# Queries, keys and gates of eight retention heads computed as Strassen pairs in a stage of their own and kept in DRAM, in a one-core decoder layer

## The chip, the cores and the metric

The kernel runs on one core of one Trainium2 chip. The metric is the device time of one execution in microseconds (us); lower is better. Times before: 1721.08, 1719.35 and 1719.22 us, median 1719.35.

## What is computed

One layer over 512 prompt tokens and 8 sequences of 8 sample tokens, T = 576 columns in all, with D = 1024 channels. Between two SwiGLU FFNs stands the token mix, which is what the change touches:

```python
z = h @ w_in                       # 1024 x 10240
u, v, q, k, rv, rg, ga, gb = jnp.split(z, SPLIT_POINTS, axis=-1)
u = gelu(u); v = layer_norm(gelu(v))
o_a = u * chunk_spatial_mix(v, gm_ws, gm_bs)
qh, kh = rotary(q), rotary(k) * DK ** -0.5          # 8 heads of 128
o_r, S_new = retention(qh, kh, rv, S0)              # values: 8 heads of 256
o_b = head_rms(o_r) * silu(rg)
merged = sigmoid(ga) * (o_a @ w_a) + sigmoid(gb) * (o_b @ w_b)
x = x + g2 * (merged @ w_o)
```

So q, k, ga and gb are 8 column blocks of 128 each and rg is 16: 48 blocks of `w_in` that all multiply the same normalised, modulated input.

## The kernel before, in words

Channels lie on the 128 partitions and tokens along the free dimension; T is worked in two halves of H = 288 columns. All data is fp32. A product is made of three matmuls, high times high, high times low and low times high, from operands that ACT (high part, a cast) and DVE (low part, a subtraction) split; `proj` (L516 to L526, matmul at L522) makes a 128 x 288 result out of 8 chunks of 128 channels that way, 24 matmuls. A weight block of 128 columns, `load_w`, is one 512 KB load on SP's queue, an ACT cast (L141) and a DVE subtraction (L142).

The program runs in this order:

- **The first FFN.** Its gate and up products go through `Weights`, `Plain` and `Pair`: a pair of weight blocks (gate and up) with both token halves is a 2 x 2 block product, and Strassen's scheme makes it with 7 products of 12 matmuls (L679) in place of 8. The operands (`Operands`) hold the needed sums of the input's blocks. `Plain` uses 8 products and serves the first two strips, while those sums are still being made; `Pair` serves the others. `ada_rest` (matmuls L265) makes the conditioning vectors a strip at a time in the background.
- **The entry to the token mix** (`last_down1`). Its steps stand in a written order, the string `INTO_MIX`. The last down products of the FFN interleave with the RMS norm of the new input, and `Modulate` (L448 to L493) turns it into the operands X, high and low, of all products in the token mix. Head 0's first blocks start here.
- **The heads**, the loop of 8 over `project` (L1196), `core` and `out_b`. `project` makes q, k and two rg blocks of a head with `proj` (8 calls, 192 matmuls), then the values (L1236: 96 matmuls of 128 x 256, L1244 for the sample tokens). `rotary` (L1186 to L1189) takes q and k out of PSUM on DVE and adds on POOL. `core` (L1278 to L1408) is the retention: it is a generator that is started, ticked by other code's products and finished, so that its small matmuls fall between the large ones of the next head's `project` and of `out_b`. It ends with the head's norm: L1377 and L1378 copy and square, L1380 adds, `split` (L149, L150) makes high and low, L1402 sums over partitions with a matrix of ones, L1406 and L1407 multiply by the gate and the norm. `out_b(h-1)` makes the 8 blocks of `w_b` (96 matmuls) and DVE adds each into `acc` in SBUF (L1421).
- **The gated branch.** `values(0)`, `values(1)` (L1452), a layer norm, then `mix(g)` (L1560, L1564) between the `gate_u` products, with the eight `gate_b` blocks filling in; a mix ends in L1566 and L1570 on DVE, L1574 on POOL, and `split`.
- **The merge.** x1 comes back from DRAM (L1604), the eight ga blocks are made, then `w_a`, then `w_o` in the written order `INTO_FFN2`, which also starts the second FFN with the same `Plain` and `Pair`.

All DMAs are issued on SP's queue; POOL and ACT issue none. The scheduler of the tile framework keeps each engine's program in the order of the code, apart from where generators are ticked.

Of the kernel before, what the change touches and what calls it, by code (L numbers as in the profile page):

```python
# [15 lines left out]
P = 128  # L16
# [15 lines left out]
NSLOT = 28  # L32
# [5 lines left out]
xt0 xt1 xc0 xt2 xc1 xt3 xc2 xt4 xc3 s5 xt5 xc4 r5 r50 r51 r52 xt6 dg xc5 xt7 xc6 rw xS  # L38
xc7 rr xr0 xr1 mm0 xr2 M0 tr0 xr3 mm1 m0 nh0 s0 M1 nl0 b00 tr1 b01 m1 wh0 tx0 b10 s1 b11
wl0 N11h0 N11h1 N11l0 N1h0 N11l1 mm2 tx1 N1l0 N1h1 h0a0 T2a1 M2 N1l1 nh1 T2a0 wh1 nl1  # L40
tr2 sn0 h1a0 m2 wl1 b20 b21 s2 B21h2 T2b0 B22h2 h0a1 B21l2 T2h0 N3c0 N4c0 N3h0 T2l0 N4h0
N3l0 mm3 N4l0 sn1 B22l2 M3 tr3 h1a1 m3 b30 s3 b31 B21h3 T2b1 p2ah B21l3 p2S h0b1 B22h3
p2bh N4c1 T2h1 p2bl N4h1 T2l1 p2al h0b0 N3c1 B22l3 N3h1 N4l1 N3l1 h1b0 e0s0 e0s1 e0m0
e0m1 h1b1 e1a0 p2Sh e1t0 e1s0 p2Sl e1m0 p2U Gh0 P1 e1t1 p2V e1a1 p2Uh P2 Gl0 e1s1 p2Ul
P1s P5 e1m1 Gh1 P6 Gl1 P5s P6s
"""
INTO_MIX = """
D00 D01 rs00 Wh2 sq00 ad00 Wl2 D10 rs01 px0 Wh3 sq01 ad01 Wl3 D11 rs10 sq10 ad10 Wh6 D20
rs11 Wl6 px1 sq11 ad11 D21 Wh7 rs20 sq20 Wl7 ad20 D30 rs21 Wh4 px2 sq21 Wl4 ad21 D31
rs30 sq30 ad30 Wh5 Wl5 D40 rs31 px3 sq31 wh0 D50 ad31 rs40 sq40 wl0 ad40 D60 rs50 sq50  # L50
wh1 ad50 wl1 D70 rs60 sq60 wh2 ad60 D41 rs70 xa60 wl2 sq70 xa70 ad70 rd0 rs41 D51 wh3
px4 rq0 wl3 sq41 ad41 q00 D61 rs51 q10 px5 sq51 q20 t00 t60 t10 hi00 D71 t70 t20 hi10
lo00 hi20 ad51 lo10 hi60 t30 hi70 lo20 hi30 B00 t40 rs61 hi40 rs71 px6 B10 sq61 lo40 px7
lo30 sq71 ad61 lo70 B20 xa61 t50 xa71 ad71 hi50 B30 lo60 lo50 rd1 B40 rq1 q01 B50 q11
q21 t11 up0 B60 t01 hi11 t21 hi01 lo11 t71 B70 hi21 um0 t61 hi71 lo01 R0 uh00 t41 uh01
ul00 ud0 lo21 hi41 ul01 t31 uc00 up1 uc01 t51 hi31 lo41 hi51 lo31 hi61 um1 lo51 uh10
lo61 ud1 ul10 uh11 lo71 uc10 ul11 uc11
"""
INTO_FFN2 = """
W00 W01 Wh2 rs00 sq00 ad00 Wl2 W10 Wh3 rs01 px0 Wl3 sq01 ad01 W11 Wh4 rs10 sq10 Wl4 ad10  # L60
W20 Wh5 rs11 px1 Wl5 sq11 ad11 W21 Wh6 rs20 sq20 Wl6 ad20 W30 Wh7 rs21 px2 sq21 Wl7 ad21
# [14 lines left out]
def layer_kernel(ctx: ExitStack, tc: tile.TileContext, a):  # L76
# [17 lines left out]
    now = {"xa": xa, "wraw": None, "whl": None}  # L94
    turn = {"wraw": 0, "whl": 0}
# [18 lines left out]

    def weight(tag, shape, dt, bufs):
        turn[tag] += 1
        own = now[tag] is not None and turn[tag] % (bufs + 1) == 0
        return (now[tag] if own else wp).tile(
            [P] + shape, dt, tag=tag, name=nm(tag), bufs=1 if own else bufs
        )  # L120

    def raw4(shape):
        return weight("wraw", shape, F32, 3)

    def whl(shape):
        return weight("whl", shape, F32R, 4)
# [668 lines left out]
    class Pair(Weights):  # L795
# [29 lines left out]
        def Sl(self):  # L825
            self.put_lo(("s3", "s1"))
# [1010 lines left out]
```

## Time and profile before

| | |
|---|---|
| median of three runs | 1719.35 us |
| the profiled execution, its own time | 1718.67 us |
| its span in the trace | 1716.6 us |
| granted TensorE clock, mean | 0.996 |
| busy: PE, DVE, ACT, POOL | 1683.7, 1049.4, 686.6, 209.0 us |
| data moved by DMA | 199.52 MB, mean 116 GB/s |

The profiled execution took 1718.67 us by the same clock as the other runs; its span, from the first to the last instruction in the trace, is 1716.6 us, so 2.07 us lie around it. A row of the groups by line names line, engine, operation, the tiles out<-in, the shape and the count, then busy time in us and the mean ns of one, then the idle time of the engine ahead of them and what ended it. A row of the windows is start:end and length in us, then busy us with the number of instructions of PE, of its weight loads (PEld), DVE, ACT and POOL, the granted clock, the share of the 16 DMA engines, and GB/s. A matmul's mean in a group is longer than the time that it adds, since matmuls are pipelined: busy time over count is the pace.

### The profile page before, as it was taken

What the parts mean: (1) busy time and instruction counts of PE and PEld (TensorE: products, weight loads), DVE (VectorE), ACT (ScalarE), POOL (GpSimd) and SP (SyncE); (2) the same over time, 40 slices, a digit from 0 to 9 for tenths busy, and PEclk for the clock granted to TensorE, in tenths of its full rate; (3) what the DMA queues carried; (4) which work ended last, traced back from release to release, by engine and by line L of the source; (5) the groups of instructions that cost most, each with busy time, mean ns of one, the idle gap of its engine ahead of it and who ended that gap; (6) DMA issues with size and microseconds to landing.
All of it is one profiled execution on the core that took longest, in us unless ns stands there. A gap on an engine that the chain in (4) does not pass through costs nothing.

```text
span 1716.6 us, 30444 instructions
## 1 busy us (share of the span) xinstructions
PE 1683.7 (98%) x12588; PEld 1610.9 (94%) x12588; DVE 1049.4 (61%) x1758; ACT 686.6 (40%) x1137; POOL 209.0 (12%) x263
## 2 busy tenths in 40 slices
PE   7999999999999999999999999999999999999997
PEld 4879999999999999999999889999999999999997
DVE  6856847676765745745745546422547958666773
ACT  5533524335534333333333333322235525344354
POOL 0000000000421302302202101220021000000002
PEclk9999999999999999999999999999999999999999
DMA  9443444323454433444424335342330323323231
GB/s 301 132 145 98 134 139 129 99 87 95 146 163 140 142 115 125 132 123 125 149 83 143 100 115 161 103 154 75 99 103 21 87 80 92 99 84 89 86 99 56
DMA packets 279773, 199.52 MB, mean 116 GB/s; under 512 B 9801, under 2 KB 253769, under 8 KB 279634
## 3 DMA queue, kind: packets, MB, share of 16 engines
q1 hardware_dynamic: 279634, 197.58, 38.4%
q8 instruction: 98, 1.61, 0.4%
q14 instruction: 41, 0.34, 0.1%
HBM read 183.12 MB, written 14.42 MB: 115 GB/s over the span
## 4 chain that ended last, share of the span: by engine, by line
PE 88%; DVE 4%; DMA 4%; ACT 2%; issue 1%; SPq 0%; POOL 0%; POOLq 0%; DVEq 0%; ACTq 0%
PE ps L522 47%; PE ps L679 24%; PE ps L1236 5%; PE ps L1452 3%; PE ps L265 2%; DMA wraw<-in_w_down_dram 1%; DMA ada<-in_w_ada_dram 1%; DVE whl L707 1%; PE ps L1366 1%; PE ps L1244 1%; PE ps L1328 1%; DMA xa<-in_w_ada_dram 1%; ACT whl L697 1%; PE ps L1372 1%; PE ps L1344 0%
## 5 line engine op out<-in xcount | busy, mean ns | idle before, releaser
L522 PE MATMUL ps<-xa,whl 128*128 128x288 f32 x2784 | 378.4, 295 | 0.5 <-DVE whl L142 0.3
L522 PEld LDWEIGHTS ps<-xa,whl 128*128 128x128 f32 x2784 | 370.9, 188 | 7.6 <-issue 3.4
L679 PE MATMUL ps<-xa,whl 128*128 128x288 f32 x2064 | 292.8, 296 | 1.9 <-ACT whl L697 1.0
L679 PEld LDWEIGHTS ps<-xa,whl 128*128 128x128 f32 x2064 | 279.1, 188 | 10.5 <-issue 2.5
L142 DVE TENSOR_TENSOR whl<-wraw,whl 128x1024 fp32r<-128x1024 f32 x100 | 126.2, 1270 | 212.4 <-ACT whl L141 208.4
L522 PE MATMUL ps<-c,wd 128*128 128x288 f32 x1824 | 246.7, 295 | 0.0
L522 PEld LDWEIGHTS ps<-c,wd 128*128 128x128 f32 x1824 | 243.2, 188 | 2.6 <-issue 1.7
L679 PE MATMUL ps<-xs,whl 128*128 128x288 f32 x1680 | 239.7, 296 | 1.6 <-ACT sn L688 1.4
L679 PEld LDWEIGHTS ps<-xs,whl 128*128 128x128 f32 x1680 | 228.5, 188 | 7.5 <-ACT sn L688 4.9
L522 PE MATMUL ps<-c,whl 128*128 128x288 f32 x1368 | 194.9, 298 | 0.0
L522 PEld LDWEIGHTS ps<-c,whl 128*128 128x128 f32 x1368 | 184.1, 188 | 2.7 <-DVE S L1391 0.8
L141 ACT CAST whl<-wraw 128x1024 fp32r<-128x1024 f32 x100 | 104.0, 1046 | 107.3 <-PE ps L522 47.6
L509 POOL TENSOR_TENSOR x<-x,s 128x64 f32<-128x64 f32 x72 | 34.4, 478 | 909.4 <-DVE s L508 909.2
L503 DVE SCALAR_TENSOR_TENSOR x<-ps,gate,x 128x288 f32<-128x288 f32 (+1 forms) x128 | 61.5, 483 | 135.3 <-PE ps L522 134.9
L697 ACT CAST whl<-sum 128x1024 fp32r<-128x1024 f32 x80 | 84.0, 1050 | 86.3 <-DVE sum L832 58.2
L707 DVE TENSOR_TENSOR whl<-sum,whl 128x1024 fp32r<-128x1024 f32 x80 | 98.0, 1225 | 30.2 <-ACT whl L697 28.2
L697 ACT CAST whl<-wraw 128x1024 fp32r<-128x1024 f32 (+1 forms) x84 | 70.6, 841 | 98.5 <-PE ps L679 84.8
L1236 PEld LDWEIGHTS ps<-whl,xa 128*128 128x128 f32 x768 | 94.1, 194 | 5.1 <-DVE whl L142 3.4
L1236 PE MATMUL ps<-whl,xa 128*128 128x256 f32 x768 | 95.6, 286 | 3.2 <-DVE whl L142 3.2
L909 ACT CAST wd<-wraw 128x640 fp32r<-128x640 f32 (+2 forms) x58 | 45.3, 782 | 123.6 <-PE ps L522 116.7
L707 DVE TENSOR_TENSOR whl<-wraw,whl 128x1024 fp32r<-128x1024 f32 (+1 forms) x84 | 81.2, 967 | 9.5 <-ACT whl L697 9.1
L688 ACT COPY sn<-ps 128x288 f32<-128x288 f32 x126 | 50.1, 398 | 59.2 <-PE ps L679 57.7
(264 smaller groups left out, 1835.2 us busy)
## 6 DMA issues: line engine op xcount, KB each, us to landing
wraw<-in_w_in_dram SPq DMA_DIRECT2D x80, 512.0 KB
ada<-in_w_ada_dram SPq DMA_DIRECT2D x56, 512.0 KB
wraw<-in_w_gate_dram SPq DMA_DIRECT2D x88, 256.0 KB
wraw<-in_w_up_dram SPq DMA_DIRECT2D x88, 256.0 KB
wraw<-in_w_down_dram SPq DMA_DIRECT2D x32, 384.0 KB
wraw<-in_w_down_dram SPq DMA_DIRECT2D x32, 320.0 KB
S<-in_state_ret_dram SPq DMA_DIRECT2D x32, 256.0 KB
wraw<-in_w_b_dram SPq DMA_DIRECT2D x16, 512.0 KB
```

Of the source, the lines that this page charges most:

```text
L141: ACT.copy(out=hi, in_=raw)
L142: (eng or DVE).tensor_tensor(out=lo, in0=raw, in1=hi.bitcast(F32), op=ALU.subtract)
L503: DVE.scalar_tensor_tensor(out=x[:, o:o + w], in0=ps[:, :w], scalar=g[:, c, 0:1], in1=x[:, o:o + w], op0=ALU.mult, op1=ALU.add)
L509: return lambda: POOL.tensor_tensor(out=x[:, NP:T], in0=x[:, NP:T], in1=u, op=ALU.add)
L522: PE.matmul(ps[:, :H], lhsT=s[:, k, c0:c0 + P], rhs=m[:, HALF[h]], start=k == 0 and z == 0, stop=k == kc - 1 and z == 2,)
L679: PE.matmul(ps[:, :H], lhsT=s[:, j * P:(j + 1) * P], rhs=m[:, j, :], start=fresh and j == 0 and z == 0, stop=j == 3 and z == 2, skip_group ...
L688: ACT.copy(out=t, in_=ps[:, :H])
L697: ACT.copy(out=hl[:, 0], in_=src)
L707: DVE.tensor_tensor(out=hl[:, 1], in0=src, in1=hl[:, 0].bitcast(F32), op=ALU.subtract)
L909: ACT.copy(out=hl[:, 0], in_=self.raw[c])
L1236: PE.matmul(ps[:, :DV], lhsT=s, rhs=m, start=i == 0, stop=i == 23)
L1452: PE.matmul(ps, lhsT=s, rhs=m[:, kx % 2, :], start=kx == 0 and z == 0, stop=kx == KC - 1 and z == len(terms) - 1,)
```

## The change

The 48 blocks q, k, rg, ga and gb are made as 24 pairs in a stage between the first FFN and the heads. The first two pairs (rg of heads 0 and 1) are `Plain2`, 96 matmuls each; the other 22 are `Pair2`, 84 each. `INTO_MIX` starts the first three of them the way `INTO_FFN2` starts an FFN. A finished block is a tile of 128 x 576 that POOL stores to DRAM (`qkd`, `rgd`, `gad`, `gbd`). The operands of the values are remade in the stage from x1 and the norm's row, both stored to DRAM in the entry (16 DMAs on ACT's queue for x1) and fetched again by POOL; `ada_rest(10..17)` moves into the stage. A head fetches q and k (each also with its partition halves swapped) and rg by SP; DVE and POOL make the rotary on 576 columns in SBUF. `out_b(h)` runs two heads later, ACT copies its sums out of PSUM, and for heads 1 to 7 POOL adds them to `accd` in DRAM with an accumulating DMA; `out_b(7)` is in the loop of mixes. `gates_of` fetches ga, gb and `accd` for `w_a`. The `gate_b` and ga products of the old merge are gone. A pair's sums are made in place in the raw weight tiles, in both FFNs as well. Counted over the program, matmuls of 128 x 288 go from 10116 to 9852, DVE instructions from 1760 to 1798, ACT from 1129 to 1382, and POOL from 268 to 345, 113 of those DMAs of 128 x 576.

The diff, cut to its core:

```diff
-NSLOT = 28
+NSLOT = 33
+NSLOT2 = 7
+SSLOT = 11
...
     class Pair(Weights):
         def S(self):
-            self.sum = now["raw"].tile([P, 2, 512], F32, tag="sum", name=nm("sum"), bufs=1)
-            DVE.tensor_tensor(
-                out=self.sum, in0=self.q[:, 1:2].broadcast_to([P, 2, 512]), in1=self.p, op=ALU.add
-            )
+            DVE.tensor_tensor(out=self.p[:, 1], in0=self.q[:, 1], in1=self.p[:, 1], op=ALU.add)
+            DVE.tensor_tensor(out=self.q[:, 1], in0=self.q[:, 1], in1=self.p[:, 0], op=ALU.add)
...
+    def stream(p, begun=False):
+        if not begun:
+            p.splits()
+            p.p1()
+            p.p1s()
+            p.p2()
+        behind()
+        p.e2()
+        if not begun:
+            p.p5()
+            p.p5s()
+            p.p6()
+            p.p6s()
+        p.p3()
+        p.p7()
+        held.append(p.p4)
...
+    class Kept:
+        def post(self, i, h, src):
+            if self.func:
+                ACT.activation(out=self.out(i, h), in_=src, func=self.func)
+            elif src.tensor is not self[i].tensor:
+                ACT.copy(out=self.out(i, h), in_=src)
+            self.left[i] -= 1
+            if not self.left[i]:
+                POOL.dma_start(out=self.dst(i), in_=self[i])
...
+            steps[f"sp{c}{h}"] = lambda c=c, h=h: nc.scalar.dma_start(out=x1d[:, c, HALF[h]], in_=xs[c][:, HALF[h]])
...
+    start(operands_of_values(), 4.0)
+    start(ada_rest(range(10, 18), 8.0), 9.0)
+    for w in (
+        [qk(hd) for hd in range(1, HEADS)] + [rg(hd) for hd in range(2, HEADS)]
+        + [gb(c) for c in range(0, KC, 2)] + [ga(c) for c in range(0, KC, 2)]
+    ):
+        stream(pair2(w))
+    finish()
...
+    def fetch(hd):
+        rope, t = tks["rope"], []
+        for i in range(2):
+            src = qkd[:, 2 * hd + i]
+            x, y = slot([P, T]), slot([P, T])
+            nc.sync.dma_start(out=x, in_=src)
+            nc.sync.dma_start(out=y[0:64], in_=src[64:128])
+            nc.sync.dma_start(out=y[64:128], in_=src[0:64])
+            t.append((x, y))
+        rg = [slot([P, T]) for _ in range(2)]
+        for e in range(2):
+            nc.sync.dma_start(out=rg[e], in_=rgd[:, 2 * hd + e])
+        for x, y in t:
+            DVE.tensor_tensor(out=x, in0=x, in1=rope[:, 0], op=ALU.mult)
+            DVE.tensor_tensor(out=y, in0=y, in1=rope[:, 1], op=ALU.mult)
+            POOL.tensor_tensor(out=x, in0=x, in1=y, op=ALU.add)
+        return t[0][0], t[1][0], rg
...
+    def out_b(hd, OB, j):
+        wb = load_w(a["w_b"][0], 2 * hd, 2, j * 512, 512)
+        for c in range(4):
+            t = slot([P, T])
+            for h in range(2):
+                ps = proj(wb, OB, h, kc=2, c0=c * P)
+                ACT.copy(out=t[:, HALF[h]], in_=ps[:, :H])
+                tick(cost(2))
+            dst = accd[:, 4 * j + c, :]
+            if hd == 0:
+                nc.sync.dma_start(out=dst, in_=t)
+            else:
+                POOL.dma_start(out=dst, in_=t, accum_op=ALU.add)
...
     for hd in range(HEADS):
-        mine = project(hd)
-        OB = []
-        gen = core(hd, *mine, OB)
-        if prev is not None:
-            finish(prev[0])
-            start(gen, 1.0)
-            out_b(hd - 1, prev[1])
+        if hd == 0:
+            rv, rvs = values_of(hd)
+            q, k, gates = fetch(hd)
         else:
-            start(gen, 1.0)
-        prev = gen, OB
+            q, k, gates = fetch(hd)
+            rv, rvs = values_of(hd)
+        if hd > 1:
+            for j in range(2):
+                out_b(hd - 2, OBs[hd - 2], j)
+        if prev:
+            finish(prev)
+        OBs.append([])
+        prev = core(hd, q, k, gates, rv, rvs, OBs[hd])
+        start(prev, 0.5)
...
+    def gates_of(c):
+        t = [slot([P, T]) for _ in range(3)]
+        for d, src in zip(t, (gad, gbd, accd)):
+            nc.sync.dma_start(out=d, in_=src[:, c])
+        POOL.tensor_tensor(out=t[2], in0=t[2], in1=t[1], op=ALU.mult)
```

How the change moves instructions, at three places. The first is PE at the end of head 0's core. In the kernel before (L1387 the state's products, L1402 the sums for the norm, L522 the next head's projection):

```order
L1387 MATMUL ps_5718<-c_5537,c_5543 128x256 x2
L1387 MATMUL ps_5723<-c_5537,c_5543 128x256 x2
L1387 MATMUL ps_5728<-c_5537,c_5544 128x256 x2
L1387 MATMUL ps_5733<-c_5537,c_5544 128x256 x2
L522 MATMUL ps_5738<-xa_4536,whl_5455 128x288 x6
L522 MATMUL ps_5738<-xa_4537,whl_5455 128x288 x6
L522 MATMUL ps_5738<-xa_4538,whl_5455 128x288 x6
L522 MATMUL ps_5738<-xa_4539,whl_5455 128x288 x6
L1402 MATMUL ps_5768<-c_5714,onesr 128x288
L1402 MATMUL ps_5768<-c_5715,onesr 128x288
L1402 MATMUL ps_5787<-c_5714,onesr 128x288
L1402 MATMUL ps_5787<-c_5715,onesr 128x288
```

In the changed kernel (L1452 the state's products, L1467 the sums for the norm, L1295 the values of the next head):

```order
L1452 MATMUL ps_8783<-c_8599,c_8605 128x256 x2
L1452 MATMUL ps_8788<-c_8599,c_8605 128x256 x2
L1452 MATMUL ps_8793<-c_8599,c_8606 128x256 x2
L1452 MATMUL ps_8798<-c_8599,c_8606 128x256 x2
L1467 MATMUL ps_8807<-c_8779,onesr 128x288
L1467 MATMUL ps_8808<-c_8779,onesr 128x288
L1295 MATMUL ps_8859<-whl_8851,xx_5394 128x256 x6
L1295 MATMUL ps_8859<-whl_8851,xx_5395 128x256 x3
L1467 MATMUL ps_8807<-c_8780,onesr 128x288
L1467 MATMUL ps_8808<-c_8780,onesr 128x288
```

The two sums of the norm stood behind 24 projection matmuls; of head 0's, the first now directly follow the state's products, and the next fill is nine value matmuls.

The second is PE at the last of the mixes. Before (L1560 and L1564 are a mix, L522 on `xa` the gate products around it):

```order
L522 MATMUL ps_12061<-xa_4539,whl_12025 128x288 x6
L1560 MATMUL ps_12089<-gws,c_10953 128x128
L1560 MATMUL ps_12089<-gws,c_10980 128x128
L1560 MATMUL ps_12089<-gws,c_11013 128x128
L1560 MATMUL ps_12089<-gws,c_11048 128x128
L1564 MATMUL ps_12094<-wd_11271,c_11067 128x64
L522 MATMUL ps_12109<-xa_4536,whl_12106 128x288 x6
L522 MATMUL ps_12109<-xa_4537,whl_12106 128x288 x6
L522 MATMUL ps_12109<-xa_4538,whl_12106 128x288 x6
```

In the changed kernel (L447 on `c_12079` is `out_b(7)`, L1633 and L1637 are the mixes, L447 on `c_12655` is the first product of `w_a`, which reads the first mixes' results):

```order
L447 MATMUL ps_13126<-c_12081,whl_13060 128x288
L1633 MATMUL ps_13135<-gws,c_12225 128x128
L1633 MATMUL ps_13135<-gws,c_12252 128x128
L1633 MATMUL ps_13135<-gws,c_12279 128x128
L1633 MATMUL ps_13135<-gws,c_12306 128x128
L1637 MATMUL ps_13140<-wd_12388,c_12325 128x64
L1633 MATMUL ps_13150<-gws,c_12225 128x128
L1633 MATMUL ps_13150<-gws,c_12252 128x128
L1633 MATMUL ps_13150<-gws,c_12279 128x128
L1633 MATMUL ps_13150<-gws,c_12306 128x128
L1637 MATMUL ps_13155<-wd_12388,c_12325 128x64
L447 MATMUL ps_13189<-c_12655,whl_13186 128x288
```

Mixes stood apart by gate products; now mixes 6 and 7 follow each other and `w_a` follows them at once.

The third is POOL in a head. Before (L1189 ends a rotary, L1406 multiplies by the gate, L1282, L1296 and L1299 prepare the sample tokens):

```order
L1189 TENSOR_TENSOR c_8534<-h_8563,h_8564 128x288
L1406 TENSOR_TENSOR h_8582<-c_8417,c_7802 128x288
L1406 TENSOR_TENSOR h_8587<-c_8418,c_7803 128x288
L1406 TENSOR_TENSOR h_8601<-c_8417,c_7802 128x288
L1406 TENSOR_TENSOR h_8606<-c_8418,c_7803 128x288
L1189 TENSOR_TENSOR c_8534<-h_8636,h_8637 128x288
L1282 TENSOR_TENSOR qdS<-c_8534,hc_8980 128x8x8
L1189 TENSOR_TENSOR c_8535<-h_8667,h_8668 128x288
L1189 TENSOR_TENSOR c_8535<-h_8698,h_8699 128x288
L1296 COPY h_9011<-c_8535 128x2x64
L1299 COPY h_9011<-c_8535 128x2x64
L1278 TENSOR_TENSOR c_9001<-c_8534,hc_8980 128x512
```

In the changed kernel (L1481 multiplies by the gate, L1498 are the accumulating DMAs of one `out_b`, L1282 ends the rotary, L1343 and L1384 are the decay products of the core):

```order
L1481 TENSOR_TENSOR c_10992<-c_10992,c_10279 128x576
L1481 TENSOR_TENSOR c_10993<-c_10993,c_10280 128x576
L1498 DMA accd<-c_11015 128x576
L1498 DMA accd<-c_11047 128x576
L1498 DMA accd<-c_11090 128x576
L1498 DMA accd<-c_11108 128x576
L1498 DMA accd<-c_11131 128x576
L1498 DMA accd<-c_11175 128x576
L1498 DMA accd<-c_11193 128x576
L1498 DMA accd<-c_11211 128x576
L1282 TENSOR_TENSOR c_11229<-c_11229,c_11230 128x576
L1343 TENSOR_TENSOR c_11307<-c_10749,hc_11286 128x512
```

POOL's arithmetic is on 576 columns where it was on 288, and the eight DMA issues of an `out_b` stand in its queue ahead of the rotary of a head.

More of the change, by code (lines that the diff above doesn't have):

```diff
@@ L1065, in layer_kernel @@
     run(BEGIN, steps)
-    x1d = dr.tile([P, KC, T], F32, name="x1d")
     n2 = Norm()
@@ new lines, in core @@
+        r = tp.tile([P, T], F32, tag="all", name=nm("r"), bufs=1)
+        u = slot([P, T])
+        for h in range(2):
+            ACT.activation(
+                out=r[:, HALF[h]], in_=ps[h][:, :H], func=AF.Abs_reciprocal_sqrt, scale=1.0 / DV, bias=epsT
+            )
+        DVE.scalar_tensor_tensor(out=u, in0=r, scalar=-0.5 / DV, in1=r, op0=ALU.mult, op1=ALU.mult)
+        for h in range(2):
+            DVE.scalar_tensor_tensor(
+                out=u[:, HALF[h]], in0=ps[h][:, :H], scalar=DV * EPS, in1=u[:, HALF[h]], op0=ALU.add, op1=ALU.mult
+            )
@@ L1707, in tok_end @@
         dst = a["y_prompt"][0, cl] if n < 4 else a["y_sample"].rearrange("b l d -> (b l) d")
[L1708 to L1711 removed]
+        out = raw4([2, 512])
         for i in range(2):
```

623 lines of the change are left out of this document (296 added, 327 removed).

## The prediction

> **What bounds the kernel now.** First the page's head, its chain of waits by engine and its DMA queues:
>
> ```profile
> span 1716.6 us, 30444 instructions
> PE 1683.7 (98%) x12588; PEld 1610.9 (94%) x12588; DVE 1049.4 (61%) x1758; ACT 686.6 (40%) x1137; POOL 209.0 (12%) x263
> PE 88%; DVE 4%; DMA 4%; ACT 2%; issue 1%; SPq 0%; POOL 0%; POOLq 0%; DVEq 0%; ACTq 0%
> q1 hardware_dynamic: 279634, 197.58, 38.4%
> ```
>
> PE is busy 98% of the span and is 88% of the chain that ended last; DMA, at 38% of its engines, is far from full. So a matmul taken away is time, as long as nothing else becomes late. Next the chain in order of time, for what one matmul costs:
>
> ```profile
> 928.02 11.51 PE ps L1236 x96
> 1166.00 130.44 PE ps L522 x984
> 1407.57 47.89 PE ps L679 x360
> ```
>
> Where nothing interrupts them, a product with `proj` runs at 130.44/984 = 132.6 ns a matmul, a Strassen product at 47.89/360 = 133.0, a values matmul at 11.51/96 = 119.9. Then the groups of PE by form, for the pace with interruptions and the idle time:
>
> ```profile
> L522 PE MATMUL ps<-xa,whl 128*128 128x288 f32 x2784 | 378.4, 295 | 0.5 <-DVE whl L142 0.3 <-DVE xa L463 0.2
> L679 PE MATMUL ps<-xa,whl 128*128 128x288 f32 x2064 | 292.8, 296 | 1.9 <-ACT whl L697 1.0 <-DVE whl L707 0.4 <-DVE h L883 0.4
> L679 PE MATMUL ps<-xs,whl 128*128 128x288 f32 x1680 | 239.7, 296 | 1.6 <-ACT sn L688 1.4
> L265 PE MATMUL ps<-ada,cs 128*32 128x512 f32 x224 | 32.9, 605 | 3.5 <-DMA ada<-in_w_ada_dram 3.5
> ```
>
> Last the windows: the start, the entry to the mix, the entry to the second FFN and that FFN in pieces of 20 us, and five loops of heads, from one head's values to those of the fifth after it.
>
> ```profile
> 0.00:20.00 20.00, 13.97 (x56) 9.78 (x56) 6.51 (x18) 10.60 (x24) 1.41 (x11) 1.00 0.91 275
> 20.00:40.00 20.00, 17.01 (x91) 7.70 (x90) 17.76 (x28) 12.21 (x19) 0.00 (x0) 0.91 1.10 319
> 440.00:460.00 20.00, 19.76 (x147) 19.41 (x146) 15.49 (x29) 10.55 (x20) 8.52 (x11) 1.00 0.44 139
> 460.00:480.00 20.00, 19.45 (x145) 19.10 (x144) 13.97 (x32) 10.52 (x27) 4.63 (x7) 1.00 0.41 138
> 480.00:500.00 20.00, 16.81 (x127) 16.61 (x126) 12.12 (x17) 6.62 (x10) 6.96 (x7) 0.91 0.57 180
> 1340.00:1360.00 20.00, 18.20 (x133) 17.49 (x132) 18.01 (x28) 10.31 (x18) 0.00 (x0) 1.00 0.19 53
> 1360.00:1380.00 20.00, 19.76 (x147) 19.29 (x146) 13.78 (x20) 10.22 (x18) 0.00 (x0) 1.00 0.34 99
> 1420.00:1440.00 20.00, 20.00 (x153) 20.00 (x152) 16.71 (x25) 11.46 (x19) 0.00 (x0) 1.00 0.31 89
> ...
> 603.84:928.02 324.18, 324.18 (x2602) 310.10 (x2602) 192.24 (x341) 115.88 (x191) 65.97 (x70) 1.00 0.41 126
> ```
>
> The heads leave PE no idle time in 324.18 us, 64.8 a loop, with DMA at 0.41 and POOL at 66 us in all; an FFN has PE at 20.00 of 20 too, with DVE at 16.71. When DMA was full (0.91 at 275 GB/s, 1.10 at 319) it moved 290 to 302 GB/s.
>
> **The change, part by part.** The sum is made against the profiled execution's own 1718.67 us; the median of the runs is 0.68 above it.
>
> *Products.* 48 blocks of 2 x 24 matmuls are 2304, at 132.6 ns 305.4 us. They become 22 x 84 + 2 x 96 = 2040, at 133.0 ns 271.4 us: **-34.1 us**. The instruction counts confirm it: 10116 to 9852 matmuls of this form, 264 fewer, and no other form changes. What feeds the stage is a pair's weights, sums and stores in 84 x 0.133 = 11.2 us, the work of an FFN strip, which keeps pace above. A POOL store frees its slot, of 11, so a landing has many us to spare: 0.
>
> *Entry to the mix.* Its waits now are 20 - 19.76, 20 - 19.45 and the hole before the first values,
>
> ```profile
> 487.34 12.81 PE L1236 MATMUL ps<-whl,xa 128*128 128x256 f32 x94 [3.19 <-DVE whl L142]
> ```
>
> together 0.24 + 0.55 + 3.19 = 4.0. The new entry has the steps of the second FFN's, whose windows leave 1.80 + 0.24 = 2.0: **-1.9**, from -4 (no waits) to +2 (also the 16 DMA issues on ACT's queue, each an SP issue's 0.34 to 0.43 by the row below, 16 x 0.37 = 6 us, of which a third shows).
>
> *The ada strips* 10 to 17 move from the heads to the stage, 16 halves of 512 KB. Behind an FFN's loads such a strip was waited for 3.5 us in four waits, by its group above, 0.9 each; a pause of 8 us between halves is shorter than before's 20. A quarter of 16 x 0.9 shows: **+4**, from 0 to 14.
>
> *The start of head 0.* The q, k and rg loads of head 0 stand on SP's queue behind the values' weights, and wait on nothing else; q and k with their swapped copies, weights and states are 2.7 MB, at 300 GB/s 9 us, and the rotary is two DVE and one POOL operation on 576 columns each, by
>
> ```profile
> L632 DVE TENSOR_TENSOR hb<-hb 128x576 f32<-128x576 f32 x16 | 11.7, 752 | 1.0 <-ACT hb L584 0.9
> L1574 POOL TENSOR_TENSOR c<-c,c 128x576 f32<-128x576 f32 x8 | 17.1, 2137 | 33.5 <-DVE c L1570 26.8 <-issue 6.6
> L1377 ACT COPY c<-ps 128x512 f32<-128x512 f32 x16 | 9.4, 587 | 21.5 <-PE ps L1372 21.5
> L1378 ACT ACTIVATE c<-c 128x576 f32<-128x576 f32 x16 | 11.0, 685 | 0.6
> L1380 DVE TENSOR_TENSOR c<-c,c 128x576 f32<-128x576 f32 x8 | 6.3, 788 | 5.6 <-ACT c L1378 5.6
> L149 ACT CAST c<-c 128x576 fp32r<-128x576 f32 x16 | 10.8, 674 | 36.6 <-POOL c L1574 26.5 <-DVE c L1380 10.2
> L150 DVE TENSOR_TENSOR c<-c,c 128x576 fp32r<-128x576 f32 x16 | 12.1, 754 | 18.4 <-ACT c L149 13.2 <-PE ps L1560 5.3
> ```
>
> 2 x 0.75 + 2.14 = 3.6 us, against 96 x 0.12 + 16 x 0.12 + 24 x 0.12 = 16.3 us of products ahead. The core's end has no fill: the first sums of the norm directly follow the state's products, and the copy, square, add, cast and subtraction between are 0.59 + 0.69 + 0.79 + 0.67 + 0.75 = 3.5 us of bare chain; before, 24 matmuls lay there. With a little of the fetch, **+5**, from 0 to 15 (the load's whole 9 us and both rotaries late).
>
> *A head's loop.* 192 x 132.6 ns = 25.4 us go, and 39.4 of 64.8 stay. What the other engines lose and gain has these rows:
>
> ```profile
> L142 DVE TENSOR_TENSOR whl<-wraw,whl 128x1024 fp32r<-128x1024 f32 x100 | 126.2, 1270 | 212.4 <-ACT whl L141 208.4 <-DMA x<-x1d 3.5
> L1421 DVE TENSOR_TENSOR c<-c,ps 128x288 f32<-128x288 f32 x112 | 46.2, 448 | 35.4 <-PE ps L522 34.8
> L688 ACT COPY sn<-ps 128x288 f32<-128x288 f32 x126 | 50.1, 398 | 59.2 <-PE ps L679 57.7 <-DVE g L782 1.3
> ```
>
> DVE has 192.24/5 = 38.4 us a loop and loses 4 x 1.27 of weights and 16 x 0.45 of sums: at most 26.1. ACT has 23.2 and takes 16 x 0.40 of copies: at most 29.6. POOL has 13.2, as many columns in fewer instructions, plus eight DMA issues. All lie below 39.4. The loads and stores of such a loop are weights of 2.1 MB, fetches of 1.8, states in and out 2.1, and 2.36 of sums with k counting how often the memory moves them: 6.05 + 2.36k MB. At k = 1 that is 8.4 MB in 39.4 us, 0.72 of 295 GB/s; at k = 2, a read and a write, 10.8 MB, 0.93. That is full enough for a load to be late once a loop: **+5** over the five loops with such sums, from 0 to 10. Before's trace has no DMA from POOL and none that accumulates. A DMA issue is bounded by SP's,
>
> ```profile
> L1604 SPq DMA_DIRECT2D x<-x1d x8: 338/430/432, 1119.1 to 1122.3; - x8
> ```
>
> 0.34 us, and by the landing of such a tile with POOL standing, about 3.4 us (an estimate: a fetch's share of a full queue), so POOL's loop is 15.9 to 40.4 us; I take the near end, since an issue is an issue, and POOL then hides. The Trainium skill ("DMA: Bandwidth & Descriptors", Issuing engines are not separate DMA queues) has all DMAs end on the same 16 engines, so that other queues save only issue time; no trace of before tests it, and by it nothing in the sum differs.
>
> POOL takes 2137 ns for 576 columns in L1574, where DVE has L1380 and L150, with two SBUF inputs each, near it. The Trainium skill ("SBUF — State Buffer", Who interferes with whom) says that a DVE instruction with two SBUF inputs blocks a GpSimd one that reads SBUF; the rotary, from PSUM before, is now of that kind. By that rule POOL's 4 x 2.1 us a loop wait for up to the DVE work beside them, 8 us more, and PE still has its 39.4 us; the row does not show how much of 2137 is such waiting.
>
> *The start of w_a.* Mixes 6 and 7 follow each other and `w_a` follows them. Its first seven chunks, 21 x 0.1326 = 2.8 us, cover POOL's two multiplications (2 x 2.14) and the split behind the second (0.67 + 0.75): 5.7 - 2.8 = 2.9, with a DVE addition from PSUM ahead, the mixes' own five matmuls beside it, **+3.2**, from 0 to 6. The gate loads queue on SP behind `w_a`'s weights: 0, to +6.
>
> *At nothing:* in-place pair sums (DVE at 16.71 of 20 covers one more operation), the layer norm's cover by four `gate_u` in place of three and a gate (25 us both ways), the late x1 load (under `w_o`'s weights). If one of these covers is gone it costs 1 to 3 us.
>
> Sum: -34.1 - 1.9 + 4 + 5 + 5 + 3.2 = **-18.8**: 1718.67 - 18.8 = 1699.9, with the median's 0.68 **1700.6 us**.
>
> **The rivals.** *A: every cover holds.* The five positive terms are zero, -36.0: 1683.4; with half of them 1692. For it: five loops of heads without a wait, and 4.0 us of waits in the three largest groups. Against it: POOL and DMA were idle there and are loaded now.
>
> *B, the slower side: the accumulating sums make DMA the bound of the heads.* If the memory's add moves its bytes k = 4 times (in small pieces, each a read and a write), a loop has 15.5 MB, at 302 GB/s 51.3 us for 39.4 of PE: five loops lose 60 in place of my 5, 1756. It decides from the loop of 44.1 us, 13.3 MB, k = 3.1: there the whole gain is gone. For it: nothing in the trace has such a transfer; against it, a read and a write are k = 2.
>
> *C: the stage goes at the FFN's mean pace*, (292.8 + 239.7)/(2064 + 1680) = 142.2 ns: 290.1 us, only -15.3, and with the other terms +15.3: no change, 1718.7 to 1719.4. For it: a pair's weight chain L697 and L707 ends PE's waits. Against it: the x360 row, ten products' worth of pairs in a row, at 133.0.
>
> That the change doesn't do what it says is no rival: the counts show the products gone.
>
> **How the numbers follow.** Forecast 0.55, its own range 1688 to 1714 (terms between their ends); A 0.18; B 0.15; C 0.12. The range leaves out half of A and most of B: 1684 to 1734. A measurement of this kernel can tell about 0.2%, 3.4 us, from no change: faster is below 1715.9, slower above 1722.8. Faster: forecast and A and little of the others, 0.75; the same, from C and B's edge, 0.07; slower, most of B, part of C, 0.18.
>
> **What would show it.** Right: matmuls of the stage at 133 ns without waits on whl; windows of heads with a DMA share of 0.7 to 0.95 and PE without idle time, at some 40 us a loop; about 4 us of waits on ada tiles; 3 us each ahead of the first norm sums and of the last chunk of the first `w_a`. Wrong: a DMA share of 1.0 in the heads with PE waiting on weights (B); PE in the stage waiting on L697 or L707's successors (C); POOL busy through a whole loop, with rotaries late.

## The result, and the profile after

The changed kernel takes **1741.22 us**, the median of four runs from 1739.34 to 1745.23, against 1719.3 us for the kernel before beside it: a ratio of 1.0128, with a 95% interval of 1.0107 to 1.0149. The forecast was 1700.6. So the change costs 22 us where 19 were to be gained. The profiled execution took 1745.23 us, with a span of 1743.5.

The head of the page, its chain of waits by engine and its DMA queues:

```profile
span 1743.5 us, 30978 instructions
PE 1667.8 (96%) x12324; PEld 1588.9 (91%) x12324; DVE 1132.4 (65%) x1796; ACT 789.9 (45%) x1374; POOL 276.3 (16%) x340
PE 77%; DMA 7%; issue 6%; DVE 5%; ACT 2%; POOL 2%; SPq 1%; POOLq 0%; ACTq 0%; DVEq 0%
q1 hardware_dynamic: 290450, 218.82, 41.9%
q0 software_dynamic: 12720, 33.63, 8.5%
```

PE was 88% of the chain and is 77%. The products did go: 264 instructions fewer on PE. But PE's busy time fell by only 15.9 us, from 1683.7, and the span grew by 26.9. The new queue q0 holds POOL's DMAs.

Where the time went is read from windows cut at the same places of both programs. In the kernel before, from the first product on the new input to the first product of `w_a`: the entry's last products, the heads, the values of the gated branch with mixes and gates.

```profile
456.46:483.76 27.30, 26.50 (x196) 25.92 (x195) 20.79 (x50) 16.29 (x36) 6.53 (x10) 1.00 0.40 136
483.76:1019.70 535.94, 532.75 (x4095) 501.46 (x4094) 303.55 (x532) 192.98 (x315) 103.16 (x112) 1.00 0.40 123
1019.70:1204.00 184.30, 182.50 (x1365) 176.53 (x1364) 77.09 (x133) 53.41 (x84) 30.64 (x24) 1.00 0.44 127
```

The same stretch of the changed kernel: the stage, heads 0 and 1, the loops of the other heads, and the gated branch up to `w_a`.

```profile
454.02:767.32 313.30, 302.38 (x2202) 282.57 (x2203) 224.59 (x341) 173.36 (x292) 33.34 (x60) 0.98 0.60 182
767.32:857.50 90.18, 79.24 (x643) 76.23 (x642) 51.44 (x73) 33.93 (x68) 32.14 (x35) 0.92 0.63 191
857.50:1098.50 241.00, 213.09 (x1732) 204.22 (x1731) 130.54 (x179) 106.27 (x235) 102.32 (x100) 0.94 0.76 197
1098.50:1230.20 131.70, 131.61 (x816) 119.15 (x814) 67.45 (x114) 50.20 (x83) 24.38 (x19) 1.00 0.47 120
```

The stretch was 747.5 us and is 776.2, 28.6 more. PE's idle time in it was 0.8 + 3.2 + 1.8 = 5.8 us and is 10.9 + 10.9 + 27.9 + 0.1 = 49.8: **+44.0**. Its busy time was 741.8 and is 726.3: **-15.4**, not -34.1, and the eighth column says why: the granted clock is 0.98 in the stage, and 0.92 and 0.94 in the heads. These means hold PE's idle time too; how much work ran slowly is read from where PE starts again after its longer waits, two in the stage, two in heads 0 and 1 and four in the loops:

```profile
639.76:649.76 10.00, 10.00 (x54) 10.00 (x55) 7.32 (x10) 4.01 (x8) 0.54 (x1) 0.69 0.37 119
761.59:767.32 5.73, 5.73 (x24) 3.04 (x25) 0.33 (x1) 0.74 (x2) 0.00 (x0) 0.70 0.69 228
789.51:799.51 10.00, 9.99 (x52) 9.45 (x53) 6.23 (x9) 2.20 (x5) 4.37 (x5) 0.67 0.51 160
816.87:826.87 10.00, 9.65 (x68) 9.27 (x68) 5.58 (x11) 3.52 (x6) 0.00 (x0) 0.84 0.91 263
913.53:923.53 10.00, 10.00 (x85) 9.49 (x86) 7.43 (x10) 0.93 (x3) 7.41 (x6) 0.73 0.24 83
958.92:968.92 10.00, 10.00 (x87) 9.49 (x88) 8.27 (x10) 1.01 (x3) 7.89 (x7) 0.78 0.40 121
1003.47:1013.47 10.00, 10.00 (x89) 9.49 (x90) 8.14 (x10) 1.01 (x3) 8.07 (x8) 0.79 0.41 127
1048.79:1058.79 10.00, 10.00 (x93) 9.49 (x94) 8.15 (x10) 1.13 (x4) 8.23 (x8) 0.83 0.35 112
```

One less the clock, times the length of the row, gives 3.1 + 1.7 = 4.8 us in the stage, 3.3 + 1.6 = 4.9 in heads 0 and 1 and 2.7 + 2.2 + 2.1 + 1.7 = 8.7 in the loops, 18.4 in all. The kernel before has 1.5 us of the kind, behind the hole at 487.34 (clock 0.85 in the ten us after it), so the clock took 16.9 us more. -15.4 - 16.9 = -32.3 is then the products' saving, near the -34.1 of the forecast. The rest of the program differs little: the first FFN ends 2.8 us earlier (415.87 for 418.68), the `w_a` products take 2.1 us longer, the tail is 1.4 shorter.

Of the 27.9 us in the loops, PE's waits after that point name one place:

```profile
PE ps L1393 <- DVE h L1377: 25.8, 4, 8.0
PE ps L1295 <- DVE c L1333: 2.1, 1, 2.1
```

The core's state product waits for a DVE operation, four times, up to 8.0 us. The chain through the first of these holes:

```profile
899.34 0.61 SPq L139
899.95 0.05 issue
900.00 11.87 DMA c<-qkd
911.87 0.02 issue
911.89 0.76 DVE c L1280
912.65 0.01 issue
912.66 0.34 DVE h L1377
```

The DVE operation that PE waits for, L1377, is not late for its own inputs. It belongs to the core of one head, and stands in DVE's queue behind L1280, the rotary of the *next* head, which waits for the fetch of q and k. DVE takes its instructions in order, so everything behind stands too:

```profile
900.72 0.22 DVE L1340 TENSOR_TENSOR scs<-ps,hc 64x64 f32<-64x64 f32 x1 [1.39 <-PE ps L1338]
911.89 0.76 DVE L1280 TENSOR_TENSOR c<-c,rope 128x576 f32<-128x576 f32 x1 [10.95 <-DMA c<-qkd]
912.66 0.72 DVE L1377 SCALAR_TENSOR_TENSOR h<-ps,hc,h 32x128 fp32r<-32x128 f32 x2
913.41 0.76 DVE L1281 TENSOR_TENSOR c<-c,rope 128x576 f32<-128x576 f32 x1
```

And the fetch is late because of its own queue. SP's instructions before it, and what the loads of the states (L1325) wait for from 886 to 906 us:

```profile
886.74 3.52 SPq L1457 DMA_DIRECT2D ut_ret_state_sample_dram<-S  x4
890.37 8.28 SPq L1325 DMA_DIRECT2D S<-in_state_ret_dram  x4
898.70 1.26 SPq L139 DMA_DIRECT2D wraw<-in_w_in_dram  x1
900.00 0.50 SPq L1272 DMA_DIRECT2D c<-qkd  x1
```

```profile
SPq L1325 <- DMA ut_ret_state_sample_dram<-S: 4.4, 3, 2.8
```

The states' loads go into the tiles that the states' stores (L1457) are still emptying, so SP spends 8.3 us on the four loads, 4.4 of them waiting for stores to land, and only then issues the fetch. That the order on DVE was so could be read beforehand, in the list of the changed kernel's DVE instructions:

```
L1340 TENSOR_TENSOR scs_10345<-ps_10343,hc_10326 64x64
L1280 TENSOR_TENSOR c_10269<-c_10269,rope 128x576
L1377 SCALAR_TENSOR_TENSOR h_10363<-ps_10360,hc_10326,h_10363 32x128 x2
L1281 TENSOR_TENSOR c_10270<-c_10270,rope 128x576
```

Windows of 10 us around that hole show the second half of its price:

```profile
890.00:900.00 10.00, 10.00 (x82) 10.00 (x81) 7.59 (x10) 6.74 (x15) 2.75 (x4) 1.00 1.10 256
900.00:910.00 10.00, 5.52 (x42) 4.83 (x41) 0.22 (x1) 2.21 (x5) 1.58 (x2) 0.94 1.09 296
910.00:920.00 10.00, 6.47 (x32) 6.32 (x33) 7.83 (x11) 0.38 (x1) 5.69 (x4) 0.55 0.49 137
920.00:930.00 10.00, 10.00 (x105) 9.24 (x105) 3.96 (x6) 5.28 (x11) 3.33 (x6) 1.00 0.28 87
```

PE's clock is 1.00 before the hole and 0.55 in the window in which it ends. The DMA engines are full in the ten us before the fetch is issued and in the ten behind that (1.10, 1.09), which leaves a rival open: that the adding DMAs are the cause, and the order only their victim.

### The profile page after: what moved, and what is told of

It reads as the page before. It is cut to its first block, busy times and chain, and to the rows that moved or that the text cites. A ratio compares the mean times of both kernels' runs of the same rounds, so it can differ in the third digit from the quotient of the medians.

```text
span 1743.5 us, 30978 instructions
## 1 busy us (share of the span) xinstructions
PE 1667.8 (96%) x12324; PEld 1588.9 (91%) x12324; DVE 1132.4 (65%) x1796; ACT 789.9 (45%) x1374; POOL 276.3 (16%) x340
## 3 DMA queue, kind: packets, MB, share of 16 engines
q10 hardware_dynamic: 2304, 2.36, 0.4%
## 4 chain that ended last, share of the span: by engine, by line
PE 77%; DMA 7%; issue 6%; DVE 5%; ACT 2%; POOL 2%; SPq 1%; POOLq 0%; ACTq 0%; DVEq 0%
PE ps L613 35%; PE ps L447 28%; PE ps L1295 3%; DMA c<-qkd 3%; PE ps L1534 3%; PE ps L269 2%; DMA ada<-in_w_ada_dram 1%; PE ps L1431 1%; PE ps L1308 1%; DMA c<-x1d 1%; DMA wraw<-in_w_down_dram 1%; PE ps L1437 1%; PE ps L1393 1%; DVE whl L641 1%; DMA ut_ret_state_sample_dram<-S 1%
## 5 line engine op out<-in xcount | busy, mean ns | idle before, releaser
L613 PE MATMUL ps<-xa,whl 128*128 128x288 f32 x3000 | 425.6, 296 | 5.2 <-DVE whl L641 2.0
L613 PEld LDWEIGHTS ps<-xa,whl 128*128 128x128 f32 x3000 | 406.4, 188 | 18.0 <-issue 6.7
L613 PE MATMUL ps<-xs,whl 128*128 128x288 f32 x2040 | 296.9, 299 | 6.3 <-ACT sn L622 6.3
L641 DVE TENSOR_TENSOR whl<-wraw,whl 128x1024 fp32r<-128x1024 f32 x192 | 234.7, 1225 | 56.4 <-ACT whl L631 48.8
L631 ACT CAST whl<-wraw 128x1024 fp32r<-128x1024 f32 x192 | 200.2, 1048 | 109.8 <-DVE wraw L755 62.4
L447 PE MATMUL ps<-c,wd 128*128 128x288 f32 x1824 | 245.7, 295 | 0.0
L447 PEld LDWEIGHTS ps<-c,wd 128*128 128x128 f32 x1824 | 242.8, 188 | 2.7 <-issue 1.7
L447 PE MATMUL ps<-c,whl 128*128 128x288 f32 x1368 | 190.3, 296 | 1.4 <-ACT c L158 1.1
L447 PEld LDWEIGHTS ps<-c,whl 128*128 128x128 f32 x1368 | 183.2, 188 | 2.5 <-ACT c L158 1.4
L151 DVE TENSOR_TENSOR whl<-wraw,whl 128x1024 fp32r<-128x1024 f32 x56 | 70.7, 1269 | 78.4 <-ACT whl L150 78.3
L1295 PE MATMUL ps<-whl,xx 128*128 128x256 f32 x768 | 103.7, 297 | 2.1 <-DVE c L1333 2.1
L1295 PEld LDWEIGHTS ps<-whl,xx 128*128 128x128 f32 x768 | 100.2, 205 | 3.2 <-DVE c L1333 2.3
L613 PE MATMUL ps<-xs,whs 128*128 128x288 f32 x480 | 70.7, 295 | 0.0
L613 PEld LDWEIGHTS ps<-xs,whs 128*128 128x128 f32 x480 | 66.2, 188 | 0.8 <-issue 0.8
L150 ACT CAST whl<-wraw 128x1024 fp32r<-128x1024 f32 x56 | 58.3, 1048 | 18.1 <-PE ps L1308 6.4
L919 DVE TENSOR_TENSOR wd<-wraw,wd 128x640 fp32r<-128x640 f32 (+2 forms) x58 | 54.1, 933 | 10.4 <-ACT wd L914 10.3
```

The lines of the kernel that those rows point to most:

```text
L150: ACT.copy(out=hi, in_=raw)
L151: (eng or DVE).tensor_tensor(out=lo, in0=raw, in1=hi.bitcast(F32), op=ALU.subtract)
L447: PE.matmul(ps[:, :H], lhsT=s[:, k, c0:c0 + P], rhs=m[:, HALF[h]], start=k == 0 and z == 0, stop=k == kc - 1 and z == 2,)
L613: PE.matmul(ps[:, :H], lhsT=s[:, j * P:(j + 1) * P], rhs=m[:, j, :], start=fresh and j == 0 and z == 0, stop=j == 3 and z == 2, skip_group ...
L631: ACT.copy(out=hl[:, 0], in_=src)
L641: DVE.tensor_tensor(out=hl[:, 1], in0=src, in1=hl[:, 0].bitcast(F32), op=ALU.subtract)
```

## Theories

**Order theory:** the heads lose their time because DVE stands on a fetch with the running core's work behind it; the fetch is late chiefly through SP's queue. **Bandwidth theory** (the prediction's rival B): the adding DMAs fill the DMA engines, and all loads land late, whatever the order. For the stage, the same question on a smaller scale: DVE stands 11.4 us there on x1 chunks that POOL fetches, again with weight splits behind.

## The experiments

Two helpers are used: `keep_in_program_order` holds an instruction behind the one that the code issued before it on the same engine, and `in_order` holds one behind another.

### The rotary behind the running core's work (e1)

```diff
-            DVE.tensor_tensor(out=x, in0=x, in1=rope[:, 0], op=ALU.mult)
-            DVE.tensor_tensor(out=y, in0=y, in1=rope[:, 1], op=ALU.mult)
+            tc.keep_in_program_order(DVE.tensor_tensor(out=x, in0=x, in1=rope[:, 0], op=ALU.mult))
+            tc.keep_in_program_order(DVE.tensor_tensor(out=y, in0=y, in1=rope[:, 1], op=ALU.mult))
...
-            q, k, gates = fetch(hd)
+            f = fetch(hd)
             rv, rvs = values_of(hd)
+            q, k, gates = turned(f)
```

`turned` is the second half of `fetch`, the rotary, now called after the values.

> Only the order on DVE changes: the four rotary multiplications of a head stand behind the values' last addition, so behind the running core's operations. Order theory (DVE stands on the fetch of q and k with the core's L1377 behind it, and PE waits for that): the 25.8 us of PE idle time ahead of L1393 go, and with them most of the 12.8 us that the lower granted clock costs in these loops: 1741 - 39 = 1702 us. Bandwidth theory (the accumulating sums fill the DMA engines and all loads land late): the loops stay at some 45 us, the wait moves to the rotary's readers: 1735 to 1741.

Measured: **1707.5 us**, ratio 0.9914 (0.9898 to 0.9931). Four loops of heads, from the end of one head's values to the fifth:

```profile
872.20:1019.60 147.40, 147.40 (x1250) 142.80 (x1249) 99.25 (x132) 75.01 (x165) 78.93 (x72) 1.00 0.91 226
```

PE has no idle time, the clock is 1.00, a loop is 36.8 us where three whole loops with a hole took 44 to 47, and the DMA engines do the same work at 0.91. Moving four instructions on one engine turned a loss of 22 us into a gain of about 15 against the kernel before. The loops' holes were DVE's order. The whole stretch of the loops, 241.0 us in the changed kernel, is now

```profile
854.15:1058.48 204.33, 204.33 (x1732) 197.51 (x1731) 134.68 (x181) 106.80 (x236) 106.83 (x99) 1.00 0.91 231
```

That is 36.7 us less: the 27.9 of holes and 8.8 of slow clock, as the windows above had it. The 12.8 in the expectation came from the mean clock, idle time included, and was too much, which is part of why 1702 was not reached.

### The fetch ahead of the states' loads (e2)

```diff
+            if j == 0 and hd + 1 < HEADS:
+                in_order([last[hd + 1], ld])
```

Here `ld` is the state's load and `last` the last load of a head's fetch, which the code issues before the core of the head ahead.

> Only the order on SP's queue changes: the fetch of the next head's q, k and gates stands ahead of the states' loads, which wait for the states' stores. Order theory: the fetch is issued about 10 us earlier in a loop and lands before DVE comes to it: the 25.8 us of holes and the clock behind them go, 1700 to 1710 us, if the slots of the fetch are free by then. Bandwidth theory: the same bytes in the same loop, 1735 to 1741.

Measured: **1721.81 us**, ratio 1.0003 (0.999 to 1.0017): level with the kernel before, and by the ratios a little over half of what e1 gains on the changed kernel. The holes at L1377 are gone, but PE's waits in the loops now read:

```profile
PE ps L1417 <- DMA S<-in_state_ret_dram: 8.0, 8, 1.2
PE ps L1301 <- DVE c L1341: 1.8, 1, 1.8
```

With the fetch first, the states' loads are late, and the product on them waits twice a loop, and in the ten us behind such a pair of waits the granted clock is 0.83 (912.53 to 922.53). So SP's queue does set which load is late, as the order theory has it, but its 1700 to 1710 took the states' loads for free. The bandwidth theory's 1735 to 1741 is clear of it.

### The sums stored without adding (e3), and that with the rotary mended (e8)

```diff
-                POOL.dma_start(out=dst, in_=t, accum_op=ALU.add)
+                POOL.dma_start(out=dst, in_=t)
```

> The sums over the heads are left out: w_b's results are stored to DRAM by POOL without adding. Order theory: fewer bytes let the fetch land somewhat earlier, at most 2 to 3 us in each of four loops: 1725 to 1741 us. Bandwidth theory with an add that moves its bytes several times: the holes of the loops go, 1700 to 1705 us.

Measured: **1709.23 us**, ratio 0.9915 (0.9894 to 0.9936). This is a miss for the order theory as I had put it: without the adds, but with DVE's order as in the changed kernel, nearly all is gained that e1 gained. The trace shows how: SP's state loads took 4.32 us in place of 8.28, since they waited for the stores ahead of them 0.8 us in place of 4.4, the fetch left at 895.49 in place of 900.00, and DVE came to it nearly in time:

```profile
903.54 0.76 DVE L1280 TENSOR_TENSOR c<-c,rope 128x576 f32<-128x576 f32 x1 [2.40 <-DMA c<-qkd]
```

So both are needed for a hole: an order that makes DVE stand, and DMA traffic that makes the fetch late by more than PE's cover. Whether the adds hold the loops up by themselves is what e8 tells, the same edit on top of e1:

> As e1, and the sums over the heads are left out: w_b's results are stored without adding. Order theory: with DVE's order mended, the loops are PE's own 36.8 us with either kind of transfer: 1707 us as e1, and only the share of the DMA engines falls. Bandwidth theory: e1 is still held by the adds, 1700 or less. The difference of DMA share at equal loop times prices one adding transfer: twice a store by the prediction's k = 2.

Measured: **1705.64 us**, ratio 0.9918 (0.9899 to 0.9937), not to be told from e1. The same four loops:

```profile
872.20:1019.60 147.40, 147.40 (x1250) 142.80 (x1250) 98.73 (x132) 75.02 (x165) 67.36 (x72) 1.00 0.71 234
```

The same 147.40 us with and without adds: bandwidth alone does not bound these loops. The DMA share is 0.71 where it was 0.91, so adding costs 0.20 x 147.4/4 = 7.4 us of all 16 engines in a loop. A plain store of the same 2.36 MB takes about 7.8 us at the 302 GB/s of the start's window, so an adding DMA costs about 1.9 stores; at e8's own rate (234 GB/s for a share of 0.71) it is 2.0. Both are estimates.

### The x1 chunks fetched one ahead (e4), and both edits (e5)

```diff
+        nxt = fetched(0)
+        yield 6.0
         for c in range(KC):
-            t = slot([P, T])
-            POOL.dma_start(out=t, in_=x1d[:, c])
+            t = nxt
+            if c + 1 < KC:
+                nxt = fetched(c + 1)
             yield 6.0
```

> In the stage alone: each x1 chunk for the values' operands is fetched one chunk ahead. Order theory, for the stage (DVE stands 11.4 us on x1 chunks with weight splits and snaps' readers behind): PE's 5.2 us of waits on L622 and the 1.1 us on L641 go with some 4 us of clock: 1731 to 1734 us. Rival (the stage is held by ACT's and DVE's own work, or by the ada strips): no change, 1739 to 1742.

Measured: **1736.28 us**, ratio 1.009 (1.0072 to 1.0109), 5 us off the changed kernel by the medians and 6.5 by the ratios, where 7 to 10 were expected. The stage shrank from 313.3 to 304.2 us in the profiled execution, and PE's idle time in it from 10.9 to 6.2. DVE still stands on x1 chunks, 13.5 us in six waits, but at other places, where PE waits less for it.

> The two edits of e1 (rotary behind the running core's work on DVE) and e4 (x1 chunks fetched one ahead) together. Order theory, with two separate places: the gains add, 33 and 5 us off the changed kernel: 1701 to 1704 us, beside 1707 for the first alone. If DMA bandwidth were what is left, the faster stage would give nothing: 1706 to 1708.

Measured: **1701.08 us**, ratio 0.9885 (0.9869 to 0.9901): 5 us below e1's ratio. The gains add, as two separate places should.

### One hole put back (e11)

As e6 below, with the rotary of head 5 alone where the changed kernel has it:

```diff
+            if hd == 5:
+                q, k, gates = turned(f, False)
             rv, rvs = values_of(hd)
-            q, k, gates = turned(f)
+            if hd != 5:
+                q, k, gates = turned(f)
```

`False` leaves out the pin that e1 put on the rotary.

> As e6, with the rotary of head 5 alone put back to where the changed kernel has it, ahead of the running core's L1377 of that kernel on DVE. Order theory: one hole of 5 to 8 us returns in one loop and costs 3 to 4 us more in granted clock: 8 to 12 us above e6, 1708 to 1712. If a hole needs the loops before it to be late too (bandwidth that adds up over the heads): 0 to 3 us above e6.

Measured: **1710.52 us**, ratio 0.994 (0.9925 to 0.9955), 0.0059 above e6's 0.9881, or 10 us. The one hole of the heads' loops:

```profile
939.54 1.19 PE L1413 MATMUL ps<-c,c 128*128 128x256 f32 x2 [8.42 <-DVE h L1397]
```

(L1413 and L1397 are L1393 and L1377 of the changed kernel.) That loop is 47.4 us where its neighbours are 36.8: of the 10.6 us, 8.4 are the hole and 2.2 the clock behind it, where 5 to 8 and 3 to 4 were expected. No loop ahead of it was late, so the traffic does not have to build up over the heads.

### Head 0 (e6, e9, e10) and the start of w_a (e7)

e6 is e5 with head 0's state loads held behind its fetch; e9 frees head 0's rotary from the pin; e10 starts head 0's core later; e7 is e6 with `out_b(7)` behind mixes 6 and 7.

```diff
+            if j == 0 and hd == 0:
+                in_order([last[0], ld])
...
-            q, k, gates = turned(fetch(hd))
+            q, k, gates = turned(fetch(hd), False)
...
-        start(prev, 0.5)
+        start(prev, 0.5 if hd else 9.0)
...
-        elif g < 6:
-            out_b(HEADS - 1, OBs[HEADS - 1], g - 4)
+        elif g > 5:
+            out_b(HEADS - 1, OBs[HEADS - 1], g - 6)
```

> As e5, and head 0's state loads stand behind its fetch of q and k on SP's queue. Theory that head 0's 5.5 us hole is the fetch queued behind 1 MB of states: 3 us of it go, and about 2 us of clock behind it: 1697 to 1700 us. Rival (the fetch waits for the memory of the stage's pools, which come free with the last products of the stage): it lands no earlier, 1701 to 1704.

Measured: **1699.86 us**, ratio 0.9881 (0.9866 to 0.9896). The time lies where the theory had it, but not for its reason: the hole ahead of head 0's scores is 5.5 us as in e1, and the ratio is not to be told from e5's. Here the rotary is pinned behind the values' last addition; when DVE comes to it, it waits for the fetch 0.35 us in e5 and not at all in e6. So under the pin the state loads do not hold it.

> As e6, with head 0's rotary alone free again to stand ahead of the values' last addition on DVE. Theory that in e6 the pin itself held head 0's rotary back: the hole ahead of the first score products falls from 5.5 to 2 to 3 us, 3 to 5 us off e6 with the clock: 1695 to 1697. Rival (head 0's q and k land no sooner, whatever the order): 1699 to 1701 as e6.

Measured: **1698.06 us**, ratio 0.9863 (0.9844 to 0.9882). The hole is 3.9 us in place of 5.5; the gain of 2 to 3 us is at the edge of what the intervals tell. e2, where head 0's rotary is free and the state loads stand behind its fetch as well, has the same 3.9. With the rotary free and three state loads ahead of the fetch, it is 6.0 in the changed kernel and 7.4 in e4. So without the pin the state loads do hold the fetch.

> As e9, and head 0's core starts later among the next head's values, behind some 90 value matmuls in place of 24. Theory (head 0's hole is want of cover): the hole ahead of the score products goes altogether, but the core's tail then has less fill, so that the 2.7 us ahead of the norm sums stay or grow to 4: 1692 to 1697. Rival (the tail loses what the head gains): 1697 to 1701.

Measured: **1698.45 us**, ratio 0.9864 (0.9846 to 0.9883). The hole is gone, and the core's tail has 1.9, 1.4 and 3.8 us in its place. What the head gains the tail loses, as the rival said.

> As e6, and the two halves of the last head's w_b stand behind mixes 6 and 7 instead of 4 and 5, so that 48 products lie between the last mix and w_a. Theory of the prediction's last term (w_a waits for the last mixes): its 1.4 us of waits and the 0.6 beside them go: 2 us below e6. Rival (the sums of that head now reach memory too late for the gates of w_a): as much or more is lost in w_a: equal or above e6.

Measured: **1700.02 us**, ratio 0.9883 (0.9866 to 0.99), the same as e6. The waits ahead of `w_a`, 1.4 us, are gone from the trace, but 1.0 and 0.8 us of new ones stand among the last mixes and `out_b(7)`, so nothing is gained; and `w_a` does not wait for late sums, as the rival had it.

The fastest of these by its ratio, e9, is 1.4% faster than the kernel before, with all of the computation (e3 and e8 leave the sums over the heads out).

## Why the prediction was wrong

- **Products, -34.1: right to some 5 us.** The stage's longest unbroken row of the chain and the window of the stage with its product line alone:

```profile
459.96 32.23 PE ps L613 x240
```

```profile
454.02:767.32 313.30, 283.71 (x2040) 276.33 (x2040) 0.98 0.60 182
```

Unbroken, a product matmul takes 32.23/240 = 134.3 ns, for 133.0 assumed. In the mean over the stage it is 283.71/2040 = 139.1, under rival C's 142.2; but by the same measure before's were 378.4/2784 = 135.9 and not 132.6, and 2304 x 135.9 - 283.7 = 29.4, to which the 4.8 us of slow clock in the stage are to be added. Rival C compared a mean with an unbroken run.
- **A head's loop, +5: the step that failed.** It added up each engine's busy time and the DMA share, found all of them below PE's loop, and asked only whether a load would be late, not what stands behind the instruction that waits for it. For head 0 I had looked at the queue; for the loops I had not looked at DVE's. Measured: 27.9 us of holes and 8.8 of clock, 36.7, all of it gone in e1. Of its parts the rest held: DMA share 0.91 in e1, in a loop of 36.8 us, where 0.93 of 39.4 was worked out for k = 2, an add that costs about 1.9 stores, no engine above the loop. The loop itself is 36.8 us, not 39.4: before's 64.8 held ada strips, 8.5 + 2.4 us on PE in five loops, that the change moves to the stage.
- **Rival B** had the right side and the right resource, and the wrong mechanism: full DMA engines did not bound the loops (e8), they made one fetch late enough for a bad order to show (e3). Its point of decision, k = 3.1, was never reached.
- **No term for the clock.** A hole was costed at its length; in the ten us in which the hole of 8 us ended the clock was 0.55, and the work behind it took 2.7 us longer. The Trainium skill ("TensorE: Matmul & The Clock Gate", What's actually happening) says that an idle window of some 3.4 us halves the clock until a busy window has passed. The 0.55 agrees, and so do the ten us behind the stage's hole of 3.4 us, at 0.69:

```profile
639.76 6.13 PE L613 MATMUL ps<-xs,whl 128*128 128x288 f32 x24 [3.40 <-ACT sn L622]
```

But shorter holes cost clock here too, and not by their length alone: one of 1.99 us in e11's stage was followed by ten us at 0.83 and the two of about 1 us in e2's loops by 0.83, while behind one of 2.28 us in e1's stage the clock stayed at 1.00.

- **The stage: the x1 fetches were costed at nothing**, as stores were, though DVE waits for them: 11.4 us of waits, and 5 to 6.5 us of time by e4, and by e5 against e1.
- **Head 0, +5:** 6.0 + 3.2 + 1.7 = 10.9 us of holes and 4.9 of clock. The sum had the rotary at 3.6 us, that of q or k alone; the scores need both, 5.8 by the same rows, and it took 6.5 in e6 with the fetch landed (DVE from 775.16, POOL to 781.63). In the changed kernel the first operation also stood 11.5 us on the fetch, which has three state loads ahead of it. How much of the hole each is worth stays open in part: 3.9 us of it are left in e9.
- **The rest** was near: the entry -2.3 for -1.9 (its waits 1.3 + 0.5 against 4.0), ada strips 2.1 + 0.7 us of waits for +4, `w_a` +2.1 for +3.2. In-place sums, costed at nothing, go with a first FFN 2.8 us shorter; no run has them alone.

With DVE's order mended the kernel takes 1707.5 us, and with the x1 fetches mended too 1698 to 1701, about the forecast. The products came true; that the total does as well is in part luck, since the loops then cost nothing where +5 was counted and are shorter than 39.4 us, while head 0 costs more than its +5.

## What to carry to other kernels

A load that is fetched ahead needs two checks: that it lands in time, and what stands behind its first reader on that reader's engine, in the list of instructions that the scheduler made. A free engine is no cover if its next instruction waits. Place the first reader of a fetch behind the work that others wait for, and count a hole of some 2 us or more on PE with the slow clock that may stand behind it, here 10.6 us for a hole of 8.4.

## What the runs showed of the hardware that was not expected

- An adding DMA of 128 x 576 is issued by POOL in 0.87 us (median; 1.17 in e1), a plain one in 0.54, against a median of 0.52 for SP's fetches of the same size (L1272); it lands in 7.7 us (median), and in 9.5 in e1. POOL does not stand for the landing. By DMA share it costs about 1.9 stores, an estimate.
- POOL's two-input operations on 576 columns in SBUF took 1.64 and 1.65 us on the mean in the heads (L1481, L1282), less than the 2.14 taken from L1574. Of the waiting beside DVE that the prediction weighed, 8 us a loop, a small part shows, and on both sides. POOL's L1282 took 1.41 to 1.43 us alone and 1.80 to 1.88 where DVE's L1280 had begun 0.16 to 0.22 us before it; a DVE L1280 begun while L1282 ran took 1.62 to 1.88 us in place of 0.76, and ended 0.61 to 0.62 us after it, five times of five in the changed kernel.
